# Scale row in two banks, a T tile in another buffer, a held v tile, a gain row by transposes, held FFN operands

## The chip, the core and the metric

The kernel runs on one core of a Trainium2 chip. A core has five engines that work through their own queues in order: TensorE (PE; PEld is its weight load), VectorE (DVE), ScalarE (ACT), GpSimd (POOL) and SyncE (SP), and sixteen DMA engines. Matmuls write to banks of PSUM, from which ACT or DVE copy. The metric is the time of one launch on the device in microseconds (us).

## What is computed

One layer on x (1024 frames of 1024 channels) and 256 memory tokens:

```python
h = rms_norm(x, mix_pre_g); proj = h @ w_in        # u 512, q, k, v 8 heads x 64, f_logit 8
y_ssm = s5_mixer(u, ...)       # per group of 16 channels a 64-dim complex state; gelu; gated linear unit
y_fox = forgetting_attention(q, k, v, f_logit)     # causal, bias from cumulated log-sigmoid
y_mix = concat(rms_norm(y_ssm, ssm_out_g), rms_norm(y_fox, fox_out_g))
x = x + rms_norm(y_mix @ w_out, mix_post_g)
x = x + rms_norm(memory_cross_attention(rms_norm(x, xa_pre_g), mem_n, wq, wkv, wo), xa_post_g)
h = rms_norm(x, ffn_pre_g)
x = x + rms_norm((silu(h @ w_gate) * (h @ w_up)) @ w_down, ffn_post_g)
```

All of it in float32.

## The kernel before

Large products keep float32 precision by splitting each operand into a high and a low part (`split`: ACT writes the high part, L113, DVE the low one, L115) and adding three matmuls (`mm3`, L122 to L124). The FFN's products (`product`, L1313) run by a scheme of seven block products in place of eight; its operands are sums and differences of weight blocks, made on POOL in `operands` (L1416) and then split.

The instructions are written as one program, partly by generators that are stepped in turns; a scheduler then sets each engine's order by its own estimates and by which tiles, banks and inputs are free. `tc.issue_after(i)` ties what is written in it behind instruction i, `tc.high_priority` draws it ahead. Tiles come from pools with a few buffers per tag: "slab" (8 KB a partition), "d", "e", "yt", "c" and "raw" for stages, "whl" for split weights. PSUM has pools g (single banks), s and x. So an edit of a tag or of one tie moves instructions of other work as well.

The stages in order, with the names that the change touches:

- Sums of x squared: TensorE against a column of ones (L231). `rsqrt_mean` (L137 to L145) makes r_x, the scale of each frame, on ACT and DVE; DVE also makes B's discretised products (L446 to L451) at that time. `row_bcast` (L171) turns r_x's columns into a row d over all partitions: eight transposes (L173) and two copies by ACT (L176). The evictions of the q and k tiles read d (L291), u is scaled by r_x (L283, L284), and so are v's (L318).
- B and C of the state space model are turned by TensorE (L459, L471) into slabs by ACT (L462, L472).
- q, k, v tiles. A v tile is written by ACT (L318) to a small buffer t, which a store takes to `v_d`. `v1` is the generator of the second half of v; one step of it is one tile of 24 matmuls of 256 columns.
- `ssm_out`: the state space output, products with the T tiles (L647) and with the states SS (L648) into a bank for each of four blocks b, gelu by ACT (L649), turnings of the result (L659). The T tiles are loaded again from `T_d` (L636) into the halves of two slabs.
- Forgetting attention: scores (L735, L736, and the mask on the diagonal, L738), the row minimum nlr by DVE (L742), turnings (L763) and values. Between them `fillers` gives TensorE other work: v1, the gated linear unit, the memory's products.
- The out projection: L1089 to L1101 normalise and scale by g_mp, the gain of the first sublayer, a row over all partitions read by a broadcast load (`gain_row`).
- FFN: block (i, m) is pair i of the hidden columns, m = 0 for gate and 1 for up. `gate_up` runs the seven products; `q.add` (L1334) adds a bank to a kept product on DVE; u2 is the sum that frees bank 2 for the last product. `finish_hid` (L1356) multiplies gate and up; `hid_sums` (L1371, four sums and differences, each stored by POOL's queue) makes operands of the down projection; `wd_sums` makes those of w_down on POOL (L1386) and stores them to `wt_d`.

Of the kernel before, what the change touches and what calls it, by code (L numbers as in the profile page):

```python
# [9 lines left out]
F32 = mybir.dt.float32  # L10
# [42 lines left out]
def layer(ctx: ExitStack, tc: tile.TileContext, a, out):  # L53
# [15 lines left out]
    def slab(shape, dt=F32R):  # L69
        return slabp.tile(shape, dt, name="slab", tag="slab")  # L70
# [23 lines left out]
    for i in range(2):  # L94
# [2 lines left out]
    pool.memset(maskb, 0.0)  # L97
    pool.affine_select(out=maskb, in_=maskb, pattern=[[-1, P]], compare_op=ALU.is_ge,
                       fill=-NEG, base=0, channel_multiplier=1)
    gains = const.tile([P, 5, KT], F32, name="gains")  # L100
    with tc.high_priority(offset=2 * 5000):
        sp.dma_start(out=gains, in_=a["gains"])
    g_mix, g_xa, g_mem, g_out, g_pre_ffn = (gains[:, i, :] for i in range(5))
# [64 lines left out]

    def row_bcast(r, n):
        rb = tt("yt", [P, n * P]) if n == 2 else tt("d", [P, n * P])  # L170
        ps = (s_ps if n > 4 else g_ps)([P, n * P])  # L171
        for j in range(n):
            pe.transpose(ps[:, j * P:(j + 1) * P], r[:, j:j + 1].broadcast_to([P, P]), ident)  # L173
        for j in range(0, n, 4):
            cs = slice(j * P, min(j + 4, n) * P)
            act.activation(out=rb[:, cs], in_=ps[:, cs], func=AF.Copy)  # L176
        return rb

    qk_d = dram.tile([8, 2, P, S], F32, name="qk_d")
# [182 lines left out]
    def ssm():  # L362
# [92 lines left out]
        for q in range(0, NP, 2):  # L455
            ps = s_ps([P, 2, 2, P])
            for qq in range(2):
                for ri in range(2):
                    pe.transpose(ps[:, qq, ri], ba[ri][:, q + qq].rearrange("p j i -> p (j i)"), ident)  # L459
            m = mi[q // 8][:, (2 * q) % 16:(2 * q) % 16 + 4, :]  # L460
            for ri in range(2):
                act.activation(out=m[:, :, ri * 64:(ri + 1) * 64].rearrange("p (q g) n -> p q g n", g=2),  # L462
                               in_=ps[:, :, ri].rearrange("p q (g n) -> p q g n", g=2), func=AF.Copy)
            yield
# [147 lines left out]
        for hf in range(2):  # L612
# [8 lines left out]
            for ri in range(2):  # L621
# [6 lines left out]
                for g2 in range(2):  # L628
                    act.activation(out=Sv[ri * 64:ri * 64 + 64, :, g2, 1:8], in_=t_[g2 * 64:g2 * 64 + 64], func=AF.Copy)
                yield  # L630
        full = [None] + [slab([P, 16, P], F32) for _ in range(2)]
        T = [[tq, full[1][:, 0:8]], [full[2][:, 0:8], full[2][:, 8:16]]]
        for hf in range(2):
            for b in range(2):
                if hf + b:
# [74 lines left out]
    def fox(yf):  # L710
# [16 lines left out]
        def scores(h, t):  # L727
            qs, ka, ncb = heads[h]
            ke = (t + 1) * P
            ps = s_ps([P, S])  # L730
            qt = qs[:, t * P:(t + 1) * P]
            for c0 in range(0, ke, 512):
                c1 = min(ke, c0 + 512)
                dg = c1 == ke
                pe.matmul(ps[:, c0:c1], qt, ka[:, 0, c0:c1], start=True, stop=False)  # L735
                pe.matmul(ps[:, c0:c1], qt, ka[:, 1, c0:c1], start=False, stop=not dg)  # L736
                if dg:
                    pe.matmul(ps[:, ke - P:ke], identb, maskb, start=False, stop=True)  # L738
            sc = tt("c")
            nlr = sm(3, "nlr")  # L740
            nm, l, rl = (nlr[:, i:i + 1] for i in range(3))
            dve.tensor_tensor_reduce(out=sc[:, :ke], in0=ps[:, :ke], in1=ncb[:, :ke], scale=1.0,  # L742
                                     scalar=3e38, op0=ALU.add, op1=ALU.min, accum_out=nm)
            last.append(act.activation(out=sc[:, :ke], in_=sc[:, :ke], func=AF.Exp, scale=-1.0, bias=nm, accum_out=l))
            dve.reciprocal(out=rl, in_=l)
            dve.tensor_scalar(out=sc[:, :ke], in0=sc[:, :ke], scalar1=rl, scalar2=None, op0=ALU.mult)
            units[h, t] = sc
# [111 lines left out]
            if next(g, "end") == "end":  # L859
                return  # L860

    ys, yf, gl, ys_stat, r_mem, gate, ssm_made, last, gw = [], [], [], [], [], [], [], [], []

    def mem_stats():
        ss = const.tile([P, 2], F32, name="ss_mem")
# [117 lines left out]


    def fillers():
        yield from v1
        yield from glu(ys)
        mem = []
        rows = out_ssm(ys)
        step(rows)  # L990
        yield
        loads = mem_load(r_mem[0], mem)
        for n in range(2 * NT - 1):
            step(rows)
            if n >= 5:
                step(loads)
            yield
        for i in range(16):
            mem_tile(i, *mem)
            yield  # L1000
        yield from rows
        yield from build_a(0)
# [37 lines left out]
    for i in range(4):  # L1040
# [2 lines left out]
        wo_read = sp.dma_start(out=w, in_=wof_d[i])  # L1043
        split(hl[:, 0], hl[:, 1], w)
        wo.append(hl)
    g_mp = gain_row(0, "d")
    VW = {}

    def value_weights(h):
# [266 lines left out]
    class Products:  # L1316
# [14 lines left out]

        def add(self, n, t, new=True):
            o = ev() if new else t
            dve.tensor_tensor(out=o, in0=self.b[n], in1=t, op=ALU.add)  # L1334
            return o

        def p1(self, w):
# [63 lines left out]
        split(o[:, 0], o[:, 1], src)  # L1401
        return o[:, 0], o[:, 1]

    def operands(i, m, engine=None):

        rw = slab([P, 2, KT, P], F32)
        for f in range(2):
            sp.dma_start(out=rw[:, f].rearrange("p k f -> p (k f)"), in_=a[GU[m]][2 * i + f])
        a11, a12, a21, a22 = rw[:, 0, 0:4], rw[:, 0, 4:8], rw[:, 1, 0:4], rw[:, 1, 4:8]
        s2, s3, s4 = (ssp.tile([P, 4, P], F32, name="ss", tag="ss") for _ in range(3))  # L1410
        s1 = a21
        def sub(o, x, y, fn=ALU.subtract):
            if engine:
                engine.tensor_tensor(out=o, in0=x, in1=y, op=fn)
            else:
                made[0] = pool.tensor_tensor(out=o, in0=x, in1=y, op=fn)  # L1416
        o = {"11": op(a11)} if i else {}
        sub(s3, a11, a21)
        o["S3"] = op(s3)
        sub(s1, a21, a22, ALU.add)  # L1420
        sub(s2, s1, a11)
        sub(s4, a12, s2)
        o["S4"] = op(s4)
        if i:
            o["12"] = op(a12)
        o["S2"] = op(s2)
        o["22"] = op(a22)
        o["S1"] = op(s1)
        return o

    def gate_up(i, m, w, q):
        q.p1(w["11"])
        p1 = q.keep(1)
        product(q.bank(4), w["S4"], "22", True)
        product(q.bank(3), w["S3"], "T3", True)
        p7 = q.keep(3)
        q.p2(w["12"])
        product(q.bank(2), w["S2"], "T2", True)
        u2 = q.add(2, p1)
        product(q.bank(3), w["22"], "T4", False)  # L1440
        product(q.bank(2), w["S1"], "T1", False)
        sums(i, m, q, p1, p7, u2, q.b[1])

    def sums(i, m, q, p1, p7, u2, c11):
# [9 lines left out]
        else:  # L1454
            for (f, t), u in c.items():
                finish_hid(i, f, t, u)
            hid_sums(i)

    seq = [(i, m) for i in range(1, NPAIR) for m in range(2)]
    ws = {}  # L1460
# [4 lines left out]
    second = x_ps([P, 512])  # L1465
    product(second, plain[1, 0][1], "21", True)
    w = operands(0, 1, dve)
    wd_sums(0)
    for f in range(2):
        plain_product(f, 1)  # L1470
    hslab("T1")
# [11 lines left out]
    product(first.bank(3), w["22"], "T4", False)  # L1483
    product(first.bank(2), w["S1"], "T1", False)
    sums(0, 1, first, p1, p7, u2, c11)
    wd_sums(1)
    for n, (i, m) in enumerate(seq):
        if n + 1 < len(seq):
            ws[seq[n + 1]] = operands(*seq[n + 1])
        gate_up(i, m, ws.pop((i, m)), Products(i, m))  # L1490
        wd_sums(n + 2)


    fst.close()
# [111 lines left out]
def lay_out(i):  # L1606
# [11 lines left out]
    def kt(g):  # L1618
        return g.reshape(-1, P).T

# [5 lines left out]
        "w_g": w_in[:, 2048:].reshape(KT, P, 8).transpose(1, 0, 2),  # L1626
        "f_bias": i["fox_f_bias"].reshape(8, 1),
        "gains": np.stack([kt(i["mix_pre_g"]), kt(i["xa_pre_g"]), kt(i["mem_g"]),
                           kt(np.concatenate([i["ssm_out_g"], i["fox_out_g"]])), kt(i["ffn_pre_g"])], axis=1),
        "post_g": np.stack([i["mix_post_g"], i["xa_post_g"], i["ffn_pre_g"], i["ffn_post_g"], i["xa_pre_g"]]),  # L1630
        "ssm_a": np.concatenate([pairs(i["ssm_a_re"]), pairs(i["ssm_a_im"])], axis=1),
        "ssm_dt": i["ssm_log_dt"].reshape(NP, 2).T,
# [30 lines left out]
```

## Time and profile before

| | |
|---|---|
| median of 3 runs | 1401.73 us (1401.56 to 1405.12) |
| the profiled execution | 1403.55 us, span 1401.8 us |
| TensorE busy | 1373.7 us, 98% of the span, granted clock 0.996 |
| DVE, ACT, POOL busy | 973.7, 646.2, 377.3 us |
| moved by DMA | 242.03 MB, mean 173 GB/s |

Times in the trace are counted from the span's start; the profiled execution's own time lies 1.8 us above its span. A row of the timeline is start, duration, engine, line, operation, output and inputs, sizes, count, and in brackets how long the engine had been idle and which instruction ended that. The products with L122 to L124, L1313 and L1591 make up nearly all of TensorE's time. In the table of slices TensorE reads 9 (90% or more) in every slice but the last.

### The profile page before, as it was taken

Reading aid. Unit: us, or ns where it says so; the run is one execution under the profiler, and the core shown is the slowest. Engines: PE = TensorE matmul, PEld = TensorE weight load, DVE = VectorE, ACT = ScalarE, POOL = GpSimd, SP = SyncE. Lnnn points to the kernel's source line nnn. Section 1 sums busy time; section 2 is a strip of 40 time slices with the busy share of each in tenths; the row PEclk is TensorE's granted clock in tenths of the full one; section 3 lists DMA queues with packets and bytes.
Section 4 is the critical chain, followed back from the end, with each engine's and each line's share of the span. In section 5 each row is a group of like instructions: output and inputs, shape, how many; then the busy total and the mean of one; then the engine's idle time right before and its main releaser. Section 6 shows DMA issues by size and latency. Waiting matters only on the chain.

```text
span 1401.8 us, 19885 instructions
## 1 busy us (share of the span) xinstructions
PE 1373.7 (98%) x7149; PEld 1144.9 (82%) x7149; DVE 973.7 (69%) x1740; ACT 646.2 (46%) x1262; POOL 377.3 (27%) x430
## 2 busy tenths in 40 slices
PE   9999999999999999999999999999999999999997
PEld 7889888879978777888888778888888888888886
DVE  7959954858667678445567998787777676655566
ACT  7373345866456547433344533333333334544441
POOL 0011110001111142001111466687666651000021
PEclk9999999999999999999999999999999999999999
DMA  6435765358662865035366354555444447965544
GB/s 218 141 105 165 216 222 139 83 155 252 184 194 83 222 194 186 0 105 169 131 219 233 135 180 157 189 188 173 160 141 163 153 151 245 355 195 195 180 166 165
DMA packets 104626, 242.03 MB, mean 173 GB/s; under 512 B 11528, under 2 KB 40200, under 8 KB 104336
## 3 DMA queue, kind: packets, MB, share of 16 engines
q1 hardware_dynamic: 86000, 178.86, 40.8%
q0 software_dynamic: 18528, 61.91, 12.4%
q8 instruction: 56, 0.92, 0.3%
q14 instruction: 42, 0.34, 0.1%
HBM read 172.05 MB, written 79.43 MB: 179 GB/s over the span
## 4 chain that ended last, share of the span: by engine, by line
PE 57%; DVE 2%; issue 1%; DMA 1%; POOL 0%; ACT 0%; DVEq 0%; SPq 0%; POOLq 0%; ACTq 0%
PE x L1313 15%; PE g L1313 12%; PE x L1591 7%; PE g L1591 7%; PE g L124 2%; PE g L122 2%; PE g L123 2%; PE x L122 2%; PE x L123 2%; PE x L124 2%; PE g L1109 1%; DVE op L115 1%; PE g L1220 0%; DVE ev L1371 0%; DMA slab<-in_w_gate 0%
## 5 line engine op out<-in xcount | busy, mean ns | idle before, releaser
L1313 PE MATMUL x<-slab,op 128*128 128x512 f32 x984 | 233.4, 389 | 0.0
L1313 PEld LDWEIGHTS x<-slab,op 128*128 128x128 f32 x984 | 184.7, 188 | 38.7 <-DVE op L115 0.5
L1313 PE MATMUL g<-slab,op 128*128 128x512 f32 x756 | 182.2, 390 | 2.3 <-DVE ev L1334 2.0
L115 DVE TENSOR_TENSOR slab<-slab 128x1024 fp32r<-128x1024 f32 (+2 forms) x96 | 115.0, 1208 | 82.9 <-ACT slab L113 81.2
L1313 PEld LDWEIGHTS g<-slab,op 128*128 128x128 f32 x756 | 141.6, 188 | 32.9 <-DVE ev L1334 2.4
L122 PE MATMUL g<-slab,whl 128*128 128x512 f32 (+1 forms) x416 | 151.7, 365 | 0.8 <-ACT slab L487 0.4
L123 PE MATMUL g<-slab,whl 128*128 128x512 f32 (+1 forms) x416 | 148.4, 357 | 0.0
L124 PE MATMUL g<-slab,whl 128*128 128x512 f32 (+1 forms) x416 | 148.4, 357 | 0.0
L113 ACT ACTIVATE slab<-slab 128x1024 fp32r<-128x1024 f32 (+2 forms) x96 | 99.0, 1037 | 102.4 <-DMA slab<-hs_d 75.2
L1591 PE MATMUL g<-slab 128*128 128x512 f32 x462 | 126.6, 389 | 0.0
L1591 PE MATMUL x<-slab 128*128 128x512 f32 x462 | 126.6, 389 | 0.0
L115 DVE TENSOR_TENSOR op<-slab,op 128x512 fp32r<-128x512 f32 x82 | 99.4, 1222 | 11.9 <-ACT op L113 11.5
L1591 PEld LDWEIGHTS g<-slab 128*128 128x128 f32 x462 | 86.7, 188 | 18.0
L1591 PEld LDWEIGHTS x<-slab 128*128 128x128 f32 x462 | 86.7, 188 | 18.0
L1386 POOL TENSOR_TENSOR wt<-wt 128x256 f32<-128x256 f32 x88 | 85.7, 974 | 30.6 <-DMA wt<-in_w_down 27.3
L113 ACT ACTIVATE op<-ss 128x512 fp32r<-128x512 f32 x63 | 39.5, 629 | 106.7 <-PE g L1313 50.9
L122 PEld LDWEIGHTS g<-slab,whl 128*128 128x128 f32 x416 | 78.7, 189 | 12.2 <-ACT whl L113 0.6
L124 PEld LDWEIGHTS g<-slab,whl 128*128 128x128 f32 x416 | 78.5, 189 | 11.6 <-DVE whl L115 0.2
L123 PEld LDWEIGHTS g<-slab,whl 128*128 128x128 f32 x416 | 78.7, 189 | 10.6
L113 ACT ACTIVATE op<-slab 128x512 fp32r<-128x512 f32 x82 | 51.1, 627 | 78.4 <-PE x L1313 40.8
L115 DVE TENSOR_TENSOR whl<-raw,whl 128x1024 fp32r<-128x1024 f32 (+2 forms) x58 | 66.0, 1144 | 20.8 <-ACT whl L113 20.5
L1416 POOL TENSOR_TENSOR ss<-slab 128x512 f32<-128x512 f32 x40 | 60.8, 1520 | 62.7 <-DMA slab<-in_w_gate 22.2
(397 smaller groups left out, 2876.2 us busy)
## 6 DMA issues: line engine op xcount, KB each, us to landing
hs_d<-ev POOLq DMA_DIRECT2D x77, 256.0 KB, 2.6
slab<-hs_d SPq DMA_DIRECT2D x35, 512.0 KB, 3.9
slab<-in_w_up SPq DMA_DIRECT2D x22, 512.0 KB, 4.4
wt<-in_w_down SPq DMA_DIRECT2D x44, 256.0 KB, 3.3
wt_d<-wt POOLq DMA_DIRECT2D x22, 512.0 KB, 3.8
slab<-in_w_gate SPq DMA_DIRECT2D x20, 512.0 KB
slab<-wt_d SPq DMA_DIRECT2D x20, 512.0 KB, 8.6
wd_d<-in_w_down SPq DMA_DIRECT2D x33, 256.0 KB, 4.7
```

The lines of the kernel that those rows point to most:

```text
L113: first = act.activation(out=hi, in_=src, func=AF.Copy, scale=1.0 if mul is None else mul)
L115: (lo_eng or dve).tensor_tensor(out=lo, in0=src, in1=hi.bitcast(F32), op=ALU.subtract)
L122: pe.matmul(ps, lh, rh, start=first, stop=False)
L123: pe.matmul(ps, lh, rl, start=False, stop=False)
L124: pe.matmul(ps, ll, rh, start=False, stop=last)
L1109: pe.transpose(tp[:, k], src[:, (k0 + k) * P:(k0 + k + 1) * P], ident)
L1313: pe.matmul(ps, x[:, k], y[:, k], start=first and k + n == 0, stop=k == 3 and n == 2, skip_group_check=not first)
L1386: pool.tensor_tensor(out=o, in0=x, in1=y, op=ALU.subtract)
L1416: made[0] = pool.tensor_tensor(out=o, in0=x, in1=y, op=fn)
L1591: pe.matmul(banks[n][j], xo[:, u, js], wo[:, v], start=ends[0] and k == 0, stop=ends[1] and k == 2, skip_group_check=onto is not None)
```

## The change

It has five parts. The row of x's scales goes to two single banks of the g pool instead of a wide one of s, each copied by ACT as soon as its four transposes are done, and B's transposes are tied behind the last transpose written so far by `row_bcast` (the list `rowed`). One of the three T halves goes to tag "d". The generator v1 runs one tile, and the rest of it is tied behind the last mask matmul written so far (the list `scored`). The gain row g_mp is made by `row_bcast` from a sixth column of gains, prepared on the host from `mix_post_g`, instead of by a broadcast load. And for the first FFN block of the loop, (1,0), the splits of the next block's operands and `hid_sums(0)` are held until u2's add, while `wd_sums` come two blocks later.

```diff
-    gains = const.tile([P, 5, KT], F32, name="gains")
+    gains = const.tile([P, 6, KT], F32, name="gains")
...
     def row_bcast(r, n):
         rb = tt("yt", [P, n * P]) if n == 2 else tt("d", [P, n * P])
-        ps = (s_ps if n > 4 else g_ps)([P, n * P])
-        for j in range(n):
-            pe.transpose(ps[:, j * P:(j + 1) * P], r[:, j:j + 1].broadcast_to([P, P]), ident)
-        for j in range(0, n, 4):
-            cs = slice(j * P, min(j + 4, n) * P)
-            act.activation(out=rb[:, cs], in_=ps[:, cs], func=AF.Copy)
+        for j0 in range(0, n, 4):
+            w = min(4, n - j0)
+            ps = g_ps([P, w * P])
+            for j in range(w):
+                rowed.append(pe.transpose(ps[:, j * P:(j + 1) * P], r[:, j0 + j:j0 + j + 1].broadcast_to([P, P]), ident))
+            act.activation(out=rb[:, j0 * P:(j0 + w) * P], in_=ps, func=AF.Copy)
         return rb
...
-                    pe.transpose(ps[:, qq, ri], ba[ri][:, q + qq].rearrange("p j i -> p (j i)"), ident)
+                    with tc.issue_after(rowed[-1].ins):
+                        pe.transpose(ps[:, qq, ri], ba[ri][:, q + qq].rearrange("p j i -> p (j i)"), ident)
...
-        full = [None] + [slab([P, 16, P], F32) for _ in range(2)]
-        T = [[tq, full[1][:, 0:8]], [full[2][:, 0:8], full[2][:, 8:16]]]
+        mid, tl = slab([P, 16, P], F32), tt("d", [P, 8, P])
+        T = [[tq, mid[:, 0:8]], [mid[:, 8:16], tl]]
...
-                    pe.matmul(ps[:, ke - P:ke], identb, maskb, start=False, stop=True)
+                    scored.append(pe.matmul(ps[:, ke - P:ke], identb, maskb, start=False, stop=True))
...
     def fillers():
-        yield from v1
+        step(v1)
+        yield
+        with tc.issue_after(scored[-1].ins):
+            drain(v1)
+        yield
         yield from glu(ys)
...
-    g_mp = gain_row(0, "d")
+    g_mp = row_bcast(gains[:, 5], KT)
...
-            dve.tensor_tensor(out=o, in0=self.b[n], in1=t, op=ALU.add)
+            self.added = dve.tensor_tensor(out=o, in0=self.b[n], in1=t, op=ALU.add)
...
-        o["S3"] = op(s3)
+        if held is None:
+            o["S3"] = op(s3)
         sub(s1, a21, a22, ALU.add)
         sub(s2, s1, a11)
         sub(s4, a12, s2)
-        o["S4"] = op(s4)
...
+        def rest():
+            if held is not None:
+                o["S3"] = op(s3)
+            o["S4"] = op(s4)
...
         u2 = q.add(2, p1)
+        with tc.issue_after(q.added.ins) if held else ExitStack():
+            for part in held:
+                part()
...
-            hid_sums(i)
+            if i:
+                hid_sums(i)
...
-    wd_sums(0)
...
-    wd_sums(1)
     for n, (i, m) in enumerate(seq):
+        held = []
         if n + 1 < len(seq):
-            ws[seq[n + 1]] = operands(*seq[n + 1])
-        gate_up(i, m, ws.pop((i, m)), Products(i, m))
-        wd_sums(n + 2)
+            ws[seq[n + 1]] = operands(*seq[n + 1], held=None if n else held)
+        if n == 0:
+            held.append(lambda: hid_sums(0))
+        gate_up(i, m, ws.pop((i, m)), Products(i, m), held)
+        wd_sums(n)
+    for n in (len(seq), len(seq) + 1):
+        wd_sums(n)
```

Lines of the changed file lie one to 24 higher: L173 is L175, L459 is L460, L471 is L472, L647 and L648 are L648 and L649, L1334 is L1339, L1356 is L1361, L1371 is L1376, L1447 is L1464.

The scheduler's order shows where things move. TensorE around the sums of x squared (L231), the turnings of r_x and those of B. Before, with a q/k tile of 48 matmuls, of which the first and last three are shown:

```order
L231 MATMUL s<-ones,d 128x1 x8
L122 MATMUL g<-slab,whl 128x512
L123 MATMUL g<-slab,whl 128x512
L124 MATMUL g<-slab,whl 128x512
...
L122 MATMUL g<-slab,whl 128x512
L123 MATMUL g<-slab,whl 128x512
L124 MATMUL g<-slab,whl 128x512
L173 MATMUL s<-ident,r_x 128x128 x8
L459 MATMUL s<-ident,slab 128x128 x12
L471 MATMUL g<-ident,slab 128x128 x4
```

Now, with the start of that tile:

```order
L231 MATMUL s<-ones,d 128x1 x8
L175 MATMUL g<-ident,r_x 128x128 x8
L460 MATMUL s<-ident,slab 128x128 x8
L122 MATMUL g<-slab,whl 128x512
L123 MATMUL g<-slab,whl 128x512
L124 MATMUL g<-slab,whl 128x512
...
L123 MATMUL g<-slab,whl 128x512
L460 MATMUL s<-ident,slab 128x128 x4
L124 MATMUL g<-slab,whl 128x512
L460 MATMUL s<-ident,slab 128x128 x4
```

The turnings of r_x and eight of B's moved ahead of the tile's 48 matmuls, other turnings of B into it.

TensorE in `ssm_out`, around the end of the first half's third block and the fourth block; the matmuls of 256 columns are those of a v tile. Before:

```order
L647 MATMUL g<-slab 128x128
L648 MATMUL g<-slab 128x128
L123 MATMUL g<-whl,slab 128x256
L124 MATMUL g<-whl,slab 128x256
...
L123 MATMUL g<-whl,slab 128x256
L124 MATMUL g<-whl,slab 128x256
L647 MATMUL g<-slab 128x128
L648 MATMUL g<-slab 128x128
```

Now, from the third block's last pair to the v tile:

```order
L648 MATMUL g<-slab 128x128
L649 MATMUL g<-slab 128x128
L648 MATMUL g<-slab 128x128
L649 MATMUL g<-slab 128x128
L648 MATMUL g<-slab 128x128
L649 MATMUL g<-slab 128x128
L648 MATMUL g<-slab 128x128
L649 MATMUL g<-slab 128x128
L648 MATMUL g<-slab 128x128
L649 MATMUL g<-slab 128x128
L123 MATMUL g<-whl,slab 128x256
```

The fourth block's pairs moved ahead of the v tile's matmuls.

DVE in the FFN's block (1,0), up to u2's add. Before, from the last products of `finish_hid`:

```order
L1356 TENSOR_TENSOR ev<-ev 128x512 x2
L115 TENSOR_TENSOR op<-ss,op 128x512
L115 TENSOR_TENSOR op<-slab,op 128x512
L115 TENSOR_TENSOR op<-ss,op 128x512
L1371 TENSOR_TENSOR ev<-ev 128x512 x2
L115 TENSOR_TENSOR op<-slab,op 128x512
L1371 TENSOR_TENSOR ev<-ev 128x512 x2
L1334 TENSOR_TENSOR ev<-g,ev 128x512
```

Now, from the same place:

```order
L1361 TENSOR_TENSOR ev<-ev 128x512 x2
L1339 TENSOR_TENSOR ev<-g,ev 128x512
L115 TENSOR_TENSOR op<-ss,op 128x512 x2
L115 TENSOR_TENSOR op<-slab,op 128x512
L115 TENSOR_TENSOR op<-ss,op 128x512
L115 TENSOR_TENSOR op<-slab,op 128x512 x2
L1376 TENSOR_TENSOR ev<-ev 128x512 x2
```

u2's add moved ahead of the splits and of `hid_sums`.

More of the change, by code (lines that the diff above doesn't have):

```diff
@@ L860, in step @@
                 return
-    ys, yf, gl, ys_stat, r_mem, gate, ssm_made, last, gw = [], [], [], [], [], [], [], [], []
+    ys, yf, gl, ys_stat, r_mem, gate, ssm_made, last, gw, scored, rowed = [], [], [], [], [], [], [], [], [], [], []
     def mem_stats():
@@ L1402, in op, with operands @@
         return o[:, 0], o[:, 1]
-    def operands(i, m, engine=None):
+    def operands(i, m, engine=None, held=None):
         rw = slab([P, 2, KT, P], F32)
@@ L1422, in operands, with gate_up @@
         sub(s4, a12, s2)
-        o["S4"] = op(s4)
[L1424 to L1428, printed above, removed]
+        def rest():
[3 more added lines that the diff above has]
+            if i:
+                o["12"] = op(a12)
+            o["S2"] = op(s2)
+            o["22"] = op(a22)
+            o["S1"] = op(s1)
+        if held is None:
+            rest()
+        else:
+            held.append(rest)
         return o
-    def gate_up(i, m, w, q):
+    def gate_up(i, m, w, q, held=()):
         q.p1(w["11"])
@@ L1456, in sums @@
                 finish_hid(i, f, t, u)
-            hid_sums(i)
+            if i:
+                hid_sums(i)
     seq = [(i, m) for i in range(1, NPAIR) for m in range(2)]
@@ L1628, in lay_out @@
         "gains": np.stack([kt(i["mix_pre_g"]), kt(i["xa_pre_g"]), kt(i["mem_g"]),
-                           kt(np.concatenate([i["ssm_out_g"], i["fox_out_g"]])), kt(i["ffn_pre_g"])], axis=1),
+                           kt(np.concatenate([i["ssm_out_g"], i["fox_out_g"]])), kt(i["ffn_pre_g"]), kt(i["mix_post_g"])], axis=1),
         "post_g": np.stack([i["mix_post_g"], i["xa_post_g"], i["ffn_pre_g"], i["ffn_post_g"], i["xa_pre_g"]]),
```

## The prediction

> **What bounds the kernel now.** I read the page's busy shares and chain, then TensorE's waits by releaser, then the timeline around each wait that the edited lines touch.
>
> ```profile
> span 1401.8 us, 19885 instructions
> ...
> PE 1373.7 (98%) x7149; PEld 1144.9 (82%) x7149; DVE 973.7 (69%) x1740; ACT 646.2 (46%) x1262; POOL 377.3 (27%) x430
> ```
>
> TensorE is busy 1373.7 of 1401.8 us, so only about 28 us can be won without taking matmuls away, and the change takes none away. Everything follows from which idle stretches of TensorE go and which come. Its waits by releaser (us in total, times, longest):
>
> ```profile
> PE g L647 <- ACT t L318: 3.2, 1, 3.2
> PE s L735 <- DVE nlr L742: 2.4, 3, 0.9
> PE g L1313 <- DVE ev L1334: 2.0, 1, 2.0
> PE g L124 <- DVE t L115: 1.9, 2, 1.4
> PE s L459 <- ACT d L176: 1.3, 1, 1.3
> ...
> PE g L122 <- DVE slab L766: 1.2, 2, 0.7
> ...
> PE g L763 <- ACT yt L790: 0.7, 1, 0.7
> PE g L122 <- ACT yt L320: 0.7, 1, 0.7
> ...
> PE g L122 <- ACT slab L487: 0.4, 1, 0.4
> ```
>
> The first five are 10.8 us, and each belongs to one part of the diff: the T tiles (L647), the last v tile (L735), the FFN's held operands (L1334), the gain row (L124) and x's scale row (L459). So the change aims at the five largest waits of its own neighbourhoods; the question is what it puts in their place.
>
> **Part A, x's scale row.** The rows from the sums of x squared (L231) to the end of B's turnings (L459):
>
> ```profile
> 61.01 1.84 PE L231 MATMUL s<-ones,d 128*128 128x1 f32 x16
> ...
> 62.69 2.29 DVE L449 TENSOR_TENSOR slab<-c 128x2048 f32<-128x2048 f32 x1
> ...
> 64.90 2.29 DVE L450 TENSOR_TENSOR slab<-c 128x2048 f32<-128x2048 f32 x1
> ...
> 67.10 1.22 DVE L115 TENSOR_TENSOR whl<-raw,whl 128x1024 fp32r<-128x1024 f32 x1
> ...
> 68.53 2.28 DVE L451 TENSOR_TENSOR slab<-slab 128x2048 f32<-128x2048 f32 x1
> ...
> 70.92 0.17 DVE L145 SCALAR_TENSOR_TENSOR r_x<-rst,rsy 128x8 f32<-128x8 f32 x1
> ...
> 71.12 3.31 ACT L283 ACTIVATE slab<-slab,r_x 128x256 f32<-128x256 f32 x8 [7.55 <-DVE r_x L145]
> ...
> 73.74 1.03 PE L173 MATMUL s<-ident,r_x 128*128 128x128 f32 x8
> ...
> 74.61 0.60 PE L459 MATMUL s<-ident,slab 128*128 128x128 f32 x4
> ...
> 75.41 1.06 ACT L176 ACTIVATE d<-s 128x512 f32<-128x512 f32 x2
> ...
> 76.52 1.19 PE L459 MATMUL s<-ident,slab 128*128 128x128 f32 x8 [1.31 <-ACT d L176]
> ...
> 82.46 0.49 PE L122 MATMUL g<-slab,whl 128*128 128x512 f32 x1
> ```
>
> What to see: the sums end at 61.01 + 1.84 = 62.85, but r_x, made from them, is written only at 71.09, because DVE works through L449, L450, L115 and L451 without a pause first. Before, 48 matmuls of a q/k tile stood between L231 and the turnings of r_x (L173) and filled 62.85 to 73.74. In the new order of TensorE the eight turnings stand directly behind L231, eight of B's tied behind them, and the 48 matmuls after those. DVE's order up to r_x is as before, and nothing there waits for TensorE. So TensorE stands from 62.85 to about 71.14: **+8.3 us**, with nothing behind it on TensorE's queue that could run.
>
> Then 16 turnings: the eight of L173 take 74.61 - 73.74 = 0.87 us, so 16 take 1.74 and end at 72.9. The row's two banks and the k tile's two are all four of the g pool, so the tile that follows waits for the first copy of the row (L176). ACT does the eight L283 first, to 74.43, then one copy at 0.53 (half of the 1.06 shown): 74.96, matmuls from about 75.05. A second wait of **+2.15 us**. What goes: from 73.74 to 82.46 before are 8.72 us for 8 of L173, 28 of L459 and 16 of L471, which at 0.109 are 5.67; 3.05 of waits is the most that can go. The 1.31 in the last row but one is certain to go, the row now having its own banks; the others are short waits for copies of B, which now lie between matmuls. I take **-2.5**, for most of them sit where the new order puts matmuls. Together +7.9.
>
> The clock is the unknown: no idle stretch of 8.3 us stands in this trace. The nearest are a wait of 3.17 us and what follows it, and one dip later:
>
> ```profile
> 199.85:203.30 3.45, 3.45 (x16) 3.39 (x16) 0.00 (x0) 1.40 (x2) 0.54 (x1) 0.52 1.02 418
> ...
> 281.60:285.20 3.60, 3.60 (x9) 2.82 (x10) 2.00 (x7) 2.52 (x5) 0.75 (x2) 0.54 0.53 146
> ```
>
> The column after the engines' busy times is the granted clock: 0.52 for 3.45 us after the 3.17 us wait. If the same happens at 71.14, the 16 turnings take about 3.4 us instead of 1.74 and end at 74.6, still before the copy at 75.05: the second wait hides the slow clock. If the slow stretch starts over or lasts twice as long, another 3.4 us at half clock follow, +1.7. Bounds 0 and +1.7; I take +0.5, nearer to the measured row. **A = +8.4**, range 7 to 11. The Trainium skill, page "TensorE: Matmul & The Clock Gate", Part 1, says that the array drops to half clock after an idle window of about 3.4 us and returns after a busy one of the same length, in a window that runs freely; the 0.52 for 3.45 us agrees, and by that rule 8.3 us of idleness would be certain to cost a half-clock stretch, which leaves 0 to +1.7 here just as the rows do.
>
> **Part B, T tiles.** The order moves the last eight pairs of L647 and L648 from behind 24 matmuls of a v tile to directly behind the others.
>
> ```profile
> 193.69 0.36 PE L123 MATMUL g<-whl,slab 128*128 128x256 f32 x1
> ...
> 199.85 0.70 PE L647 MATMUL g<-slab 128*128 128x128 f32 x2 [3.17 <-ACT t L318]
> ...
> 203.80 0.39 PE L122 MATMUL g<-whl,slab 128*128 128x256 f32 x1 [0.27 <-ACT slab L649]
> ...
> 206.78 1.04 PE L659 MATMUL g<-ident,slab 128*128 128x128 f32 x8
> ```
> ```profile
> 190.91 1.91 ACT L629 ACTIVATE slab<-b 64x896 f32<-64x896 f32 x2
> 199.32 0.47 ACT L318 ACTIVATE t<-g,r_x 128x256 f32<-128x256 f32 x1 [6.50 <-DMA qk_d<-t]
> 199.81 1.28 ACT L649 ACT_TABLE_LOAD   x1
> ```
>
> L647 waits for a bank that L318 empties, and L318 waits 6.50 us for a tile that a store still reads; gelu's table load and the gelus (L649) stand behind it. In the new order the moved pairs want a bank that the first gelu frees, and table load and gelus stand ahead of that L318 on ACT: 192.82 + 1.28 + 0.6 (a gelu: the 2.07 us of four, with their overlap) is about 194.7. TensorE is ready at 193.69 and waits about 1.0 instead of 3.2. Then the four double pairs at full clock, 1.8, the 23 and 24 matmuls of the v tiles (2.75 and 2.9): L659 at about 202.1 instead of 206.78, **-4.7**. In it are 1.7 of half clock. L318 is done at 199.8 as before, now behind the gelus, and its bank is next wanted after 202. If the short wait grows by a late gelu the gain shrinks to 3; I take **-4.4**.
>
> **Part C, the held v tile.** Its 24 matmuls now stand between the first and the second scores on TensorE, so two waits for the rows' minima nlr find work:
>
> ```profile
> 233.50 0.44 PE L735 MATMUL s<-slab,a 128*128 128x384 f32 x1 [0.57 <-DVE nlr L742]
> ...
> 235.68 0.50 PE L735 MATMUL s<-slab,a 128*128 128x512 f32 x1 [0.90 <-DVE nlr L742]
> ```
>
> 0.57 + 0.90 = **-1.5**, bounds -1.9 (with the start-up of the matmul behind each) and 0 (the softmax waits reappear two scores later).
>
> **Part D, the gain row** made by eight turnings of a gain column instead of a broadcast load.
>
> ```profile
> 499.37 2.53 POOL L1093 TENSOR_TENSOR a<-a,d 128x512 f32<-128x512 f32 x2 [16.69 <-DMA d<-in_post_g]
> ```
>
> POOL waits 16.69 us for that load, and the first rows of the out projection come late; the two waits of 1.9 us at L124 for the split of t follow from them. Added: 8 x 0.109 = 0.87 on TensorE's path, and two ACT copies of 0.53 beside matmuls. **-0.9**; bounds -1.9 and +0.9 (the waits stay).
>
> **Part E, held operands.** At the FFN's second block L1313 waits 2.0 us for u2's add (L1334), which DVE reaches only after the four sums of `hid_sums` (L1371) and splits:
>
> ```profile
> 818.21 2.92 DVE L1371 TENSOR_TENSOR ev<-ev 128x512 f32<-128x512 f32 x2
> 821.05 0.68 DVE L115 TENSOR_TENSOR op<-slab,op 128x512 fp32r<-128x512 f32 x1
> 821.65 2.92 DVE L1371 TENSOR_TENSOR ev<-ev 128x512 f32<-128x512 f32 x2
> 824.49 0.68 DVE L1334 TENSOR_TENSOR ev<-g,ev 128x512 f32<-128x512 f32 x1
> ```
>
> In the new order that add stands ahead of the held splits and of L1371, some 6 us earlier, and finds its matmuls just ended. **-2.0**. The splits held back are wanted only by the next block's second product, behind the rest of this block and a whole product. POOL's sums of w_down move two blocks later and their stores with them; on POOL's queue they still stand ahead of the stores that the down projection reads first, so I cost that at nothing. Bounds -2.2 and 0.
>
> **Sum.** +8.4 - 4.4 - 1.5 - 0.9 - 2.0 = -0.4 us. The profiled execution took 1403.55 (span 1401.8), 1.8 above the median of 1401.73; the terms are differences inside it, so I set them on the median: **1401.3 us**. All minima of the gains (B -3, C 0, D +0.9, E 0) with A at 8.4 would give 1408; all maxima (-4.7, -1.9, -1.9, -2.2) with A at 7, 1398.
>
> **Rivals.**
> (1) Slower: the clock stays at half beyond the second wait. A 128x512 matmul then takes about 0.43 us (the 281.60 row: nine in 3.60, with one gap's worth of full speed) instead of 0.23. From 23 such matmuls on, that is to about 85 us, it costs 4.6 and the kernel passes +0.3%; with the whole tile of 48 slow it is +9.6, 1411; I set 1407. For it: the idleness is 2.6 times the longest one seen. Against: after that one, full clock came back in 3.45 us. 0.12.
> (2) The third T tile, which now lies in the buffer d, lands late. It can load only when d's last reader in the q/k tiles is done, about the time of the L629 row (191), and is needed from about 204, while the transfer engines are full (share 1.02 in the 199.85 row) and L318's store of that time kept its tile for 6.50 us and more. The margin is some 6 us; if it is missed B loses up to 4: 1405. 0.12.
> (3) Faster: with TensorE 8 us behind, ACT, DVE and the transfers run ahead, and waits that the diff does not touch vanish: L487 (0.4), L320 (0.7), perhaps L766 (1.2) and L790 (0.7), and with the shifted pattern the half clock at 281.60, which costs 3.60 x 0.46 = 1.7. All are 4.7: 1396.6. From 3.8 of them on it counts as faster. Against: L766 and L790 belong to chains that start from TensorE's own scores. 0.20.
> (4) The scale row costs nothing because r_x comes earlier than in this trace: then the gains stand alone with the 2.5 of A, 1401.7 - 8.8 - 2.5 = 1390.4. Against: DVE's order up to r_x is unchanged and back to back. 0.04.
>
> **Chances.** The likeliest case has 0.50, a remainder of 0.02 is slower by causes not seen. 0.3%, 4.2 us, is about what a measurement of this kernel can tell from no change; that is below 1397.5 and above 1405.9. Faster: (3), (4) = 0.24. Slower: (1), half of (2), the remainder and the top of the likeliest case = 0.24. Same 0.52. The range 1396.5 to 1407.5 leaves out (4), the worse half of (1) and tails.
>
> **What would show it.** A: an idle stretch of about 8 us of TensorE ahead of the turnings of r_x with DVE's r_x as releaser, a second of 0.5 to 2 us for the row's copy, granted clock near a half in between, and full from 75 to 76 on. B: L318 no longer releases the T matmuls, and no half clock stands near 200 (all times there 8 us later). C, D, E: the waits for nlr in the first scores, for t's split and for u2's add are gone. I am wrong if the first stretch is under 6 us, or if the next wait in B, D or E is as long as the one that it replaces.

## The result: slower by 0.5%, and the profile after

The changed kernel took 1409.63 us in the median of six runs (1407.89 to 1413.16), the kernel before 1401.64 in as many; the ratio is 1.0052, interval 1.0031 to 1.0074. The prediction was 1401.3 with a range of 1396.5 to 1407.5. The profiled execution has a span of 1409.1 us against 1401.8.

TensorE's busy time hardly moved (1373.7 us before, 1375.4 now, in the first fence). The second fence has its waits, from the list by releaser (us in total, times, longest):

```profile
PE 1375.4 (98%) x7157; PEld 1147.9 (81%) x7157; DVE 968.5 (69%) x1740; ACT 648.8 (46%) x1264; POOL 375.8 (27%) x430
```
```profile
PE g L175 <- DVE r_x L145: 7.7, 1, 7.7
PE x L1318 <- ACT ev L1334: 6.0, 3, 5.3
PE s L736 <- DVE nlr L743: 1.3, 1, 1.3
...
PE g L648 <- ACT slab L650: 1.0, 1, 1.0
```

The waits for L318, for u2's add and for the two first nlr are gone, as forecast, and that for t's split fell from 1.9 to 0.4. The wait for r_x was forecast too. The second row was not: 6.0 us at the FFN's products (L1318, before L1313), for a copy by ACT (L1334 in the new file, `keep`).

Where the time came from is read by setting the same TensorE instruction of both traces side by side. Of each the start after a wait that both kernels have (before in the first fence, after in the second):

```profile
103.50 0.50 PE L122 MATMUL g<-slab,whl 128*128 128x512 f32 x1 [0.42 <-ACT slab L487]
...
473.89 0.50 PE L123 MATMUL x<-slab 128*128 128x512 f32 x1 [0.23 <-DVE slab L115]
...
536.12 0.50 PE L122 MATMUL g<-whl,t 128*128 128x512 f32 x1 [0.69 <-ACT t L113]
```
```profile
110.47 0.50 PE L122 MATMUL g<-slab,whl 128*128 128x512 f32 x1 [0.42 <-ACT slab L488]
...
209.44 1.04 PE L660 MATMUL g<-ident,slab 128*128 128x128 f32 x8
...
475.63 0.50 PE L123 MATMUL x<-slab 128*128 128x512 f32 x1 [0.23 <-DVE slab L115]
...
536.60 0.50 PE L122 MATMUL g<-whl,t 128*128 128x512 f32 x1 [0.88 <-ACT t L113]
```

| up to | after minus before | the part that lies there | that part alone |
|---|---|---|---|
| 103.50 | +7.0 | A, scale row | +7.0 |
| 206.78 (L659) | +2.7 | B, T tiles | -4.3 |
| 473.89 | +1.7 | C, held v tile, and the rest of attention | -0.9 |
| 536.12 | +0.5 | D, gain row | -1.3 |
| the end | +7.3 | E, FFN | +6.8 |

So in these two profiles four of the five terms came out near the forecast (+8.4, -4.4, -1.5, -0.9), and the whole miss is part E: -2.0 forecast, +6.8 measured. (The timed runs below say less for B, C and D.) The second wait at the FFN, on VectorE, ScalarE and TensorE, with GpSimd beside it:

```profile
828.96 0.68 DVE L1376 TENSOR_TENSOR ev<-ev 128x512 f32<-128x512 f32 x1
...
830.16 2.87 DVE L1376 TENSOR_TENSOR ev<-ev 128x512 f32<-128x512 f32 x1
...
833.55 4.78 DVE L1464 TENSOR_TENSOR ev<-ev 128x512 f32<-128x512 f32 x1
833.90 0.74 POOL L1391 TENSOR_TENSOR wt<-wt 128x256 f32<-128x256 f32 x1
...
834.60 1.29 POOL L1421 TENSOR_TENSOR slab<-slab 128x512 f32<-128x512 f32 x1
...
835.84 0.72 POOL L1391 TENSOR_TENSOR wt<-wt 128x256 f32<-128x256 f32 x1
...
836.52 1.25 POOL L1421 TENSOR_TENSOR ss<-slab 128x512 f32<-128x512 f32 x1
...
838.36 0.63 ACT L1470 ACTIVATE ev<-ev 128x512 f32<-128x512 f32 x1 [6.74 <-DVE ev L1464]
...
840.62 0.58 ACT L1334 ACTIVATE ev<-x 128x512 f32<-128x512 f32 x1
...
841.25 7.56 PE L1318 MATMUL x<-slab,op 128*128 128x512 f32 x22 [5.27 <-ACT ev L1334]
```

Read from below: TensorE waits 5.27 us for a bank that ACT's `keep` (L1334) must empty. On ACT that copy stands behind the silu of the block before (L1470), which waits 6.74 us for VectorE's L1464, a sum of two tiles of 128x512 in SBUF. L1464 takes 4.78 us, where the same form, two tiles in SBUF, takes 0.68 in the row of 828.96 with no GpSimd sum beside it, and it ends at 838.33, 0.56 us after GpSimd's four sums, run back to back from 833.90 to 837.77, have ended. Behind the wait TensorE's granted clock is at half:

```profile
64.40:74.60 10.20, 3.97 (x17) 3.60 (x18) 8.58 (x20) 4.16 (x10) 0.00 (x0) 0.50 0.18 51
...
839.30:846.10 6.80, 4.85 (x11) 3.84 (x12) 4.58 (x7) 2.67 (x5) 1.83 (x2) 0.50 0.45 149
```

(stretch, its length, busy time of PE, PEld, DVE, ACT, POOL, then the granted clock.) The second row costs about 2.2 us, 11 matmuls at 0.43 us instead of 0.23. The first is discussed below.

My theory after this: A costs 7 us through VectorE's late r_x; E costs 7 us, by the order (hid_sums held behind u2's add now stand ahead of L1464 on VectorE) and by GpSimd, beside which VectorE's sums of two SBUF tiles stand still. The rivals to test: that the losses are given back later, that the order alone does it, and for A that the tie or the banks do it.

### The profile page after: what moved, and what is told of

It reads as the page before. It is cut to its first block, busy times and chain, and to the rows that moved or that the text cites. A ratio compares the mean times of both kernels' runs of the same rounds, so it can differ in the third digit from the quotient of the medians.

```text
span 1409.1 us, 19900 instructions
## 1 busy us (share of the span) xinstructions
PE 1375.4 (98%) x7157; PEld 1147.9 (81%) x7157; DVE 968.5 (69%) x1740; ACT 648.8 (46%) x1264; POOL 375.8 (27%) x430
## 4 chain that ended last, share of the span: by engine, by line
PE 54%; DVE 3%; DMA 2%; issue 1%; POOL 1%; ACT 1%; SPq 0%; DVEq 0%; POOLq 0%; ACTq 0%
PE x L1318 14%; PE g L1318 10%; PE x L1612 7%; PE g L1612 7%; PE g L124 2%; PE g L122 2%; PE g L123 2%; PE x L123 2%; PE x L124 2%; PE x L122 2%; PE g L1114 1%; DVE op L115 1%; POOL wt L1391 1%; DMA wt_d<-wt 1%; DMA wt<-in_w_down 1%
## 5 line engine op out<-in xcount | busy, mean ns | idle before, releaser
L1318 PE MATMUL x<-slab,op 128*128 128x512 f32 x984 | 236.5, 392 | 6.2 <-ACT ev L1334 6.0
L1318 PEld LDWEIGHTS x<-slab,op 128*128 128x128 f32 x984 | 186.0, 189 | 46.9 <-ACT ev L1334 7.2
L1318 PE MATMUL g<-slab,op 128*128 128x512 f32 x756 | 181.9, 389 | 0.2 <-ACT op L113 0.2
L1318 PEld LDWEIGHTS g<-slab,op 128*128 128x128 f32 x756 | 141.7, 188 | 30.1 <-ACT op L113 0.8
L115 DVE TENSOR_TENSOR op<-slab,op 128x512 fp32r<-128x512 f32 x82 | 96.3, 1186 | 10.6 <-ACT op L113 10.4
L123 PEld LDWEIGHTS g<-slab,whl 128*128 128x128 f32 x416 | 78.8, 189 | 10.6
L122 PE MATMUL g<-whl,slab 128*128 128x512 f32 (+2 forms) x224 | 75.1, 346 | 1.5 <-ACT yt L320 0.7
```

Source lines behind the costliest of these rows:

```text
L115: (lo_eng or dve).tensor_tensor(out=lo, in0=src, in1=hi.bitcast(F32), op=ALU.subtract)
L122: pe.matmul(ps, lh, rh, start=first, stop=False)
L123: pe.matmul(ps, lh, rl, start=False, stop=False)
L1318: pe.matmul(ps, x[:, k], y[:, k], start=first and k + n == 0, stop=k == 3 and n == 2, skip_group_check=not first)
```

## The experiments

Ratios are to the kernel before, run beside on the same chip.

**The FFN part undone** (functions of the FFN as before; the rest of the change stays).

> The changed kernel with the FFN part (operands, hid_sums, wd_sums, gate_up) as before the change. Theory (the FFN part costs the kernel some 7 us): the two waits for ACT's keep near 831 and 841 us and the half clock behind them go, the 2.0 us wait for u2's add comes back; about 1402.5 us, 1.0006 of before. Rival (the FFN part is neutral and the loss lies in the scale row alone or is spread): above 1406 us.

1408.19 us, 1.0049 (1.0033 to 1.0065); the profiled execution was the fastest, 1404.33. The two waits for L1334 are gone. That for u2's add came back longer than before (2.0):

```profile
PE g L175 <- DVE r_x L145: 7.9, 1, 7.9
PE g L1318 <- DVE ev L1339: 2.8, 1, 2.8
```

Timed, this kernel is no better than the whole change, so the FFN part's 7 us don't show here, and by its own bound the rival stands. What is clear is only that without E the scale row's loss is not covered by B, C and D: the forecast for these four was +1.6 us, the ratio says 6.9. The next two runs separate the parts better.

**The scale row undone** (the wide tile of s for r_x, no tie).

> The changed kernel with x's scale row as before the change (one wide tile of s, no tie of B's turnings); the gain row stays made by transposes. Theory (the row costs 7.0 us, as the start of the slab matmul behind L482 moved from 102.8 to 109.8): the 7.7 us wait for r_x goes, the 1.3 us wait for the row's copy comes back; about 1402.6 us. Rival (the delay is given back later, since DVE, ACT and the transfers run ahead meanwhile): above 1405 us.

1405.79 us, 1.0036 (1.0021 to 1.0051), by the text's bound the rival's side, though 4 us under the whole change in another session. The wait for r_x is gone, the FFN's waits for L1341 (`keep` in that file) are there unchanged, 6.1 us. E alone, on top of B, C and D, keeps the kernel slow.

**Both undone**, so B, C and D alone.

> The changed kernel with both x's scale row and the FFN part as before the change; what is left is the T tile in d, the held v tile and the gain row by transposes. Theory (the terms add): 1409.6 - 7.0 - 6.9 = 1395.7 us, 0.996 of before, with the waits at the T tiles, two of the waits for nlr and the wait for t's split gone. Rival (the parts overlap, a gain in one place only lets the next wait grow): 1399 us or more.

1400.19 us, 0.9995 (0.9980 to 1.0010). With one step more this gives the timed prices, in one session: A on top of it is 1408.19 - 1400.19 = +8.0, E on top of it 1405.79 - 1400.19 = +5.6. Each is about the size that the traces show. But in the medians they do not add: together they would be 13.6 us, and the whole change lies only 8.0 above this kernel by the ratios (1.0052 against 0.9995), so E on top of A hardly shows (1.0052 against 1.0049, from two sessions). In the profiles they nearly add: the spans are 1396.1 us with neither, 1402.4 with A, 1403.9 with E and 1409.1 with both. Why the medians differ from the profiles here stays open.

The sum that was to be won is not there either: -6.5 us of B, C and D in the traces and -6.8 forecast, -0.7 timed (-2.8 to +1.4), the rival's value. Two reasons are visible. One is that the first profile of before was a longer execution than most, see the next run. The other is that the wait for u2's add is longer here than before (2.8 us against 2.0, and 0.8 for a split ahead of it), though the FFN's code is that of before: the edits further up moved the orders there, and now a product of two SBUF tiles on VectorE has three GpSimd sums beside it:

```profile
809.22 4.14 DVE L1368 TENSOR_TENSOR ev<-ev 128x512 f32<-128x512 f32 x1
...
809.58 1.30 POOL L1428 TENSOR_TENSOR ss<-slab 128x512 f32<-128x512 f32 x1
...
810.82 0.74 POOL L1398 TENSOR_TENSOR wt<-wt 128x256 f32<-128x256 f32 x1
...
811.52 1.28 POOL L1428 TENSOR_TENSOR slab<-slab 128x512 f32<-128x512 f32 x1
```

**A second profile of the kernel before.**

> The kernel before once more, for a second profile. The profiled execution of before took 1403.55 us, 15 runs since then have a median of 1400.06. Theory (it had a longer wait at the T tiles than most): the wait of L647 for L318 is under 2.5 us and no half clock stands near 200 us, so that part B's gain of 4.3 us was read from a bad execution. Rival (the profile was typical there): 3.0 us or more and a half clock of 3.4 us behind it again.

1400.07 us. The wait at the T tiles is 2.49 us, not 3.17:

```profile
PE g L647 <- ACT t L318: 2.5, 1, 2.5
```

It lies on the theory's bound, and a half clock stands behind it, though the wait is 0.7 us shorter, so neither text is right. The first execution had another half-clock stretch at 281.60, which this one has not. Up to the FFN the second profile is 3.5 us ahead of the first, and measured against it B, C and D are worth about 3 us in the traces, not 6.5. The changed kernel's profile has that stretch too (granted clock 0.51 from 283.00 to 286.40); without it they would be worth some 4.7. The profile with B, C and D alone, which has no such stretch either, starts the FFN 4.1 us ahead of this one (750.97 against 755.10) and ends 2.2 us ahead; it was the fastest of its ten executions. A half-clock stretch of 3.4 us that comes in one execution and not in the next is worth up to 1.7 us, and every part's gain that was read from one trace carries that.

**wd_sums one block later.** TensorE's, VectorE's and ScalarE's orders in block (1,0) stay those of the change.

```diff
-        wd_sums(n)
-    for n in (len(seq), len(seq) + 1):
+        if n:
+            wd_sums(n - 1)
+    for n in range(len(seq) - 1, len(seq) + 2):
         wd_sums(n)
```

> The changed kernel with one edit: wd_sums come one block later still, so that GpSimd has none of them during the FFN's block (1,0); TensorE's, VectorE's and ScalarE's orders are the same there. Theory (a VectorE sum of two tiles in SBUF stands still while GpSimd runs, and L1464 with 4.78 us is the late producer): L1464 takes under 2.2 us, the 5.3 us wait at L1318 shrinks to under 1.5, no half clock behind it, about 1403 us. Rival (the order itself is at fault: hid_sums behind u2's add stand ahead of L1464): L1464 is late anyway, the wait stays above 4 us, about 1409 us.

1411.53 us, 1.007 (1.0049 to 1.0092). The wait stayed at 5.27 us, which is the rival's value, but the run decides nothing: other sums moved into the gap, and L1464 again had four GpSimd sums beside it, of which these are the first rows:

```profile
834.64 4.78 DVE L1464 TENSOR_TENSOR ev<-ev 128x512 f32<-128x512 f32 x1
...
835.00 0.74 POOL L1391 TENSOR_TENSOR wt<-wt 128x256 f32<-128x256 f32 x1
```

**wd_sums not before the fourth block**, caught up in the later ones.

> The run before moved wd_sums by one block and the next block's sums took their place on GpSimd, so L1464 stood beside the same four GpSimd sums. Here GpSimd has no sum of wd_sums until three blocks later; TensorE's, VectorE's and ScalarE's orders in block (1,0) are those of the changed kernel. Theory (VectorE's sums of two SBUF tiles stand still while GpSimd runs): beside L1464 only two sums of operands are left, it takes 0.7 to 3 us instead of 4.78, the 5.3 us wait shrinks by as much, to 1 to 3.5. Rival (L1464's 4.78 us or its place in the order come from something else): 4.78 and 5.3 stay.

Here L1464 has two sums of operands beside it (833.17 to 834.46, and from 834.55) and none of wd_sums:

```profile
832.82 2.21 DVE L1464 TENSOR_TENSOR ev<-ev 128x512 f32<-128x512 f32 x1
...
833.17 1.29 POOL L1421 TENSOR_TENSOR slab<-slab 128x512 f32<-128x512 f32 x1
...
839.04 1.22 PE L1318 MATMUL x<-slab,op 128*128 128x512 f32 x2 [3.01 <-ACT ev L1334]
```

4.78 became 2.21 and 5.27 became 3.01, with the same order on the three other engines: 2.3 us of the wait are GpSimd's sums, and the theory's range held. What the order alone costs is not separated by this: of the 3.01 us that are left, GpSimd's sums have a part too (L1376 at 830.10 still takes 2.19 us beside one of them). The kernel as a whole took 1418.86 us, 1.0111 (1.0070 to 1.0153): with two wd_sums a block at the end the same kind of wait for `keep` came back there, larger:

```profile
1184.88 5.49 PE L1318 MATMUL x<-slab,op 128*128 128x512 f32 x12 [6.96 <-ACT ev L1334]
```

**Only the splits held** (hid_sums(0) at once; scale row as before).

```diff
-            if i:
-                hid_sums(i)
+            hid_sums(i)
...
-        if n == 0:
-            held.append(lambda: hid_sums(0))
```

> The changed kernel with x's scale row as before and hid_sums(0) not held; only the splits of the next block's operands are held behind u2's add. Theory (holding hid_sums behind u2's add is what puts them ahead of L1464): the 5.3 us wait at L1318 is gone, some wait for u2's add of up to 2 us is left, about 1400 us, 0.3 to 0.5% under the kernel with the scale row alone undone (1405.8). Rival (the held splits do it): the wait stays above 3 us and the time at 1405.

1396.15 us, 0.9947 (0.9927 to 0.9966), and once more in another session 1396.70, 0.9958 (0.9939 to 0.9976):

> The kernel with only the splits held, late wd_sums and x's scale row as before, once more. Theory (its gain is real): 0.9935 to 0.996 of before, no wait above 1 us at L1313's counterpart between 800 and 850. Rival (it came from slow runs of before in that session): 0.998 or more.

Both are within their theories' bounds or better. Against the kernel with hid_sums held (1.0036) this is 0.9%, some 12 us by the two ratios, with this edit alone. The traces show less: 6.1 us of waits and about 2.4 of half clock (12 matmuls at 0.43 us instead of 0.23) went, and the spans are 6.7 us apart (1403.9 and 1397.2), 10.6 in the repeat (1393.3). The rest is not explained. In the first profile TensorE has no wait above 0.3 us in the FFN's first blocks, neither for u2's add nor for `keep`; L1464's counterpart takes 0.68 us, with no GpSimd sum beside it until 821.17:

```profile
820.84 0.68 DVE L1471 TENSOR_TENSOR ev<-ev 128x512 f32<-128x512 f32 x1
...
821.17 1.52 POOL L1428 TENSOR_TENSOR ss<-slab 128x512 f32<-128x512 f32 x1 [2.16 <-DMA slab<-in_w_up]
```

So holding hid_sums was the faulty half of part E. What is left of it, the held splits with the late wd_sums, is worth 0.4 to 0.5% (0.9995 to 0.9958 and 0.9947), more than the 2.0 us of the forecast. One wait of 1.9 us is left at the FFN's end, in the repeat:

```profile
PE x L1325 <- ACT ev L1341: 1.9, 1, 1.9
```

**The same, with wd_sums at their old places** (the first two ahead of the loop, two ahead later).

> The changed kernel with x's scale row as before, hid_sums(0) not held and wd_sums at their old places; of the FFN part only the held splits are left. The run with hid_sums not held took 0.9947 of before and still had a wait of 2.4 us for ACT's keep at the FFN's end (1170 us) with a half clock of 3.4 us behind it, which the kernels with wd_sums at the old places do not show. Theory (late wd_sums crowd GpSimd's end and hold VectorE up there): that wait and its half clock go, 3 to 4 us less, 0.991 to 0.993 of before. Rival (the wait has another cause, or wd_sums at their old places crowd the first blocks instead): 0.995 or more, with a wait near 820 to 840 us.

1400.23 us, 0.9998 (0.9984 to 1.0012). The rival. The wait at the end is gone, but one of 4.40 us stands in the first block:

```profile
819.03 0.74 POOL L1398 TENSOR_TENSOR wt<-wt 128x256 f32<-128x256 f32 x1 [3.89 <-DMA wt<-in_w_down]
...
822.99 0.63 ACT L113 ACTIVATE op<-ss 128x512 fp32r<-128x512 f32 x1 [3.62 <-POOL ss L1428]
...
823.66 0.69 DVE L115 TENSOR_TENSOR op<-ss,op 128x512 fp32r<-128x512 f32 x1 [4.96 <-ACT op L113]
...
830.39 1.22 PE L1325 MATMUL x<-slab,op 128*128 128x512 f32 x2 [4.40 <-ACT ev L1341]
```

GpSimd waits for a weight tile of wd_sums at 819, the operand sum ss behind it is late, its split waits on ACT and VectorE, and everything behind the split waits too. So with the held splits, moving wd_sums two blocks later, which I had costed at nothing, is worth 0.4 to 0.5%; the held splits without it are worth nothing (0.9998, and 0.9995 without both). Whether the late wd_sums would pay without the held splits was not run.

**wd_sums late, caught up in two middle blocks.**

> The kernel with the held splits alone of the FFN part, late wd_sums and x's scale row as before (0.9947 of before), with wd_sums catching up by one in two middle blocks, so that they end two blocks earlier. Theory (wd_sums must be out of the first two blocks, and out of the last ones): no wait above 1 us near 820 to 840 nor near 1170, 2 to 4 us under that kernel, 0.992 to 0.994 of before. Rival (the wait at 1170 is one of a transfer that comes late anyway, or the two crowded middle blocks wait instead): 0.9945 or more.

1395.30 us, 0.9947 (0.9929 to 0.9965). No wait above 1 us is left near 820 or 1170, as the theory said; the time is the rival's, not to be told from the kernel without the catching up. This run and the two with only the splits held beat both kernels: they are the change without the scale row and without the held hid_sums.

**No tie of B's turnings** (A's banks stay).

> The changed kernel without the tie of B's turnings; the row stays in two single banks. In this order eight of B's turnings stand ahead of the turnings of r_x, both ahead of the q/k tile. Theory (what costs is that the row's turnings stand ahead of the tile's 48 matmuls, which the two banks alone bring about): TensorE waits about 7.5 us behind L231, now for VectorE's L451, and the time is that of the changed kernel, 1408 to 1412 us. Rival (the tie moves them): the wait is under 2 us and the time 1402 to 1404.

1412.38 us, 1.0063 (1.0041 to 1.0085), 0.4 us above the theory's range. TensorE waits 5.3 + 1.9 us behind L231, now at B's own turnings:

```profile
PE s L459 <- DVE rsv L139: 5.3, 1, 5.3
PE s L459 <- DVE slab L451: 1.9, 1, 1.9
```

The 7.2 us are close to the theory's 7.5. So the two banks alone pull the turnings ahead of the tile's 48 matmuls, and the tie is innocent.

**r_x ahead of B's second half on VectorE.**

```diff
-        dve.tensor_tensor(out=t_, in0=BR, in1=Ri, op=ALU.mult)
-        dve.tensor_tensor(out=u_, in0=BI, in1=Rr, op=ALU.mult)
-        dve.tensor_tensor(out=ba[1], in0=t_, in1=u_, op=ALU.add)
+        with tc.issue_after(rx_done[0].ins):
+            dve.tensor_tensor(out=t_, in0=BR, in1=Ri, op=ALU.mult)
+            dve.tensor_tensor(out=u_, in0=BI, in1=Rr, op=ALU.mult)
+            dve.tensor_tensor(out=ba[1], in0=t_, in1=u_, op=ALU.add)
```

> The changed kernel, FFN part included, with one edit: the second half of B's products (L449 to L451 before) is tied behind r_x on VectorE, so r_x comes at about 64.4 us instead of 70.9. Theory (the row's price is the wait for VectorE, not the turnings or the banks): the wait of 7.7 us shrinks to 1 to 2, a wait of 2 to 3 for the row's first copy stays since ACT still scales u first, no or a shorter half clock; 4 to 6 us less than the changed kernel, about 1404 to 1406. Rival (the delay only moves to B's turnings, which now come later): 1408 or more.

1405.96 us, 1.0035 (1.0017 to 1.0053), within the theory's 1404 to 1406:

```profile
PE g L122 <- ACT d L176: 1.5, 1, 1.5
PE g L175 <- DVE r_x L145: 1.5, 1, 1.5
```

7.7 became 1.5, and the first product behind B's and C's turnings starts 3.9 us earlier than in the changed kernel (106.60 against the row of 110.47). A half clock of 6.8 us stayed. By timing alone the gain is not clear of noise, since the interval overlaps that of the changed kernel (1.0031 to 1.0074); the trace shows that most of the row's price was the wait for VectorE.

## Why the prediction was wrong, point by point

- **A** was right in its mechanism and a little too dear: +8.4 forecast, +7.0 in the trace, +8.0 timed without E. The wait was 7.67 us (8.3 forecast; VectorE was 0.7 us earlier in that execution). The second wait, forecast at 2.15, or 0.5 with the turnings at half clock, came out at nearly nothing, because the 16 turnings did run at half clock and filled it (70.56 to 74.20, with the tile from 74.28):

```profile
70.56 1.94 PE L175 MATMUL g<-ident,r_x 128*128 128x128 f32 x8 [7.67 <-DVE r_x L145]
...
72.29 1.91 PE L460 MATMUL s<-ident,slab 128*128 128x128 f32 x8
...
73.65 1.05 ACT L176 ACTIVATE d<-g 128x512 f32<-128x512 f32 x2
```

  Rival (1), a clock that stays low, did not come: full from 74.7 on, right at the tile's first matmuls. Rival (4) is refuted, rival (3) too: nothing of the 7.0 was given back up to 135 us, though ACT and VectorE had 8 us of lead, the waits that it named are still in the list (0.4, 0.7, 1.2 and 0.7), and the half clock of 281.60 stands at 283.
- **B** was right in this trace, -4.3 for -4.4, with a wait of 1.02 us for the first gelu where 1.0 was forecast:

```profile
201.91 0.49 PE L648 MATMUL g<-slab 128*128 128x128 f32 x2 [1.02 <-ACT slab L650]
```

  Rival (2), a late T tile in d, did not come here; in two of the other profiles TensorE did wait 1.3 and 1.5 us for the load of a T tile into a slab (with B, C and D alone, and with wd_sums from the fourth block on). But the term was read from one execution; the second profile has 0.7 us less of wait to win.
- **C** was forecast at -1.5; the two waits went, and one of 0.88 us for the sums of the state space output (L240) came, so with the rest of attention it is -0.9.
- **D** was forecast at -0.9 and came to -1.3: of the 1.9 us of waits at t's split 0.4 is left.
- **E** is the step that failed in the mechanism: -2.0 forecast, +6.8 in the trace, +5.6 timed without A. "In the new order that add stands ahead of the held splits and of L1371, some 6 us earlier, and finds its matmuls just ended" was right, and the 2.0 us did go. "Nothing on the path waits there", and the bounds -2.2 and 0, were wrong: the next wait, 5.27 us for `keep`, is longer than the one that it replaced, which the prediction had named as a sign of being wrong. I followed the held splits to their readers and forgot the other held thing: four sums of hid_sums, now behind u2's add, stand ahead of L1464, and ACT's silu of L1464 stands ahead of the `keep` that frees a bank of the next block. I also put GpSimd's late wd_sums at nothing ("so I cost that at nothing"): two of the four sums beside L1464 are theirs, and without them the wait was 2.3 us shorter. And I never asked why the rows that I quoted had two VectorE sums in 2.92 us, where one takes 0.68. The reason is in the trace of before as well: a sum of SBUF tiles beside GpSimd, and one with a PSUM operand beside GpSimd:

```profile
803.07 2.11 DVE L115 TENSOR_TENSOR op<-slab,op 128x512 fp32r<-128x512 f32 x1
803.22 1.40 POOL L1416 TENSOR_TENSOR slab<-slab 128x512 f32<-128x512 f32 x1
...
804.70 1.63 POOL L1416 TENSOR_TENSOR ss<-slab 128x512 f32<-128x512 f32 x1
805.11 0.68 DVE L1334 TENSOR_TENSOR ev<-x,ev 128x512 f32<-128x512 f32 x1
```

  The first is three times as long as in quiet, the second keeps its 0.68. The Trainium skill, "GPSIMD Engine Reference", section 8, says that GpSimd shares its SBUF interfaces with VectorE and contends with VectorE instructions that have two SBUF inputs; these rows agree, and so does L1464 with 4.78, 2.21 and 0.68 us beside four, two and no GpSimd sums (the last as L1471 above).
- **The sum** is the second step that failed: it was set on the median by adding differences from one profile. Of the -6.8 us of B, C and D the timed kernel with them alone shows -0.7 (-2.8 to +1.4). Half-clock stretches differ from execution to execution: the granted clock of 15 runs of before was 0.994 to 0.999, their times 1397.74 to 1405.72. With A and E at their measured values the sum is +7.0 - 4.3 - 0.9 - 1.3 + 6.8 = +7.3, the spans' difference, and the medians differ by +8.0. That these agree is in part luck: the timed parts alone would make 8.0 - 0.7 + 5.6 = +12.9.

What stays open: how much of B, C and D is real in the median. Their traces say about 3 to 6.5 us up to the FFN, the timed kernel with them alone 0 (0.9980 to 1.0010), and the longer wait for u2's add explains 1.6 of it. And why, in the medians, E costs 5.6 us without the scale row and hardly anything with it.

## What to carry to other kernels

When a step is held back, list what stands behind it on its own engine's queue, and follow each of these through the other engines to the next bank that must come free; the held step's own readers are not enough. Before a turning, a copy or a sum is moved ahead of a block of matmuls, look when its input is really written: 48 ready matmuls stood here behind one transpose that waited 7.67 us, and none of them ran. And take a gain of a few us out of a single profile only with a second profile beside it.

## What the runs showed of the hardware that I had not expected

A VectorE sum or product of two 128x512 tiles in SBUF does not share time with GpSimd's sums but waits for a pause in them. It takes 0.68 us alone, 2.19 beside one GpSimd sum, 2.87 beside two, 4.14 beside three and 4.78 beside four, all back to back, and in each of these rows it ends 0.56 or 0.57 us after the last GpSimd sum before the pause has ended. A sum with one operand in PSUM stays at 0.68 (the row of 805.11).

After 7.67 us without work TensorE worked at half clock for 4.1 us, little longer than the 3.45 after 3.17. The slow clock began at 64.4, 1.5 us into the wait and 3.4 after the start of the 16 narrow matmuls of L231 ahead of it (61.04), and ended at 74.7, so most of its 10.2 us ran while there was nothing to slow. In the second profile of the kernel before, a wait of 2.49 us was followed by a half clock of 3.4 us as well.
